# Differential attention in three units a head instead of four, with the filling products and the mixing dealt out anew

## The chip, the cores and the metric

The kernel runs on one core of one Trainium2 chip. The time is the device time of that core in microseconds (us); lower is better.

## The reference, cut to what matters

The kernel computes a trunk of two layers for one sequence of 512 tokens with 1024 features. A layer projects the normalized input into five parts, mixes two of them over time in chunks (the gating part), runs differential attention on the other three, and joins both with `w_out`; a convolved feed-forward part follows. Attention has 4 heads, and each head has two maps of 64 columns, whose softmaxes are subtracted. Queries come in blocks of 128 and see the keys up to their own block, so the four blocks of a head have 128, 256, 384 and 512 keys.

```python
u, v_sgu, q, k, v_att = jnp.split(proj, [...], axis=-1)
u = jax.nn.gelu(u)
v_sgu = jax.nn.gelu(v_sgu)
y_sgu = sgu_mixer(u, v_sgu, ...)     # u * (w @ rmsnorm(v_sgu) + b), chunks of 128, 4 groups
...
for start in range(0, S, Q_BLOCK):   # Q_BLOCK = 128, S = 512
    end = start + Q_BLOCK
    qb = q[:, start:end]
    kb = k[:, :end]
    scores = jnp.einsum('bqhmd,bkhmd->bhmqk', qb, kb) * scale
    scores = jnp.where(mask, scores, -jnp.inf)
    p = jax.nn.softmax(scores, axis=-1)
    attn = p[:, :, 0] - lam * p[:, :, 1]
    outs.append(jnp.einsum('bhqk,bkhd->bqhd', attn, v[:, :end]))
o = rmsnorm(jnp.concatenate(outs, axis=1), subln_g) * (1.0 - lambda_init)
...
h = h + jnp.concatenate([y_sgu, y_att], axis=-1) @ w_out[l]
h = h + conv_ffn(rmsnorm(h, ffn_norm[l]), ...)
```

## The kernel before, in words

**Products.** Every large product is made of rounded parts: an operand `x` is kept as a rounded `xh` and a remainder `xl`, and three products (`h*h`, `l*h`, `h*l`) are added up in one bank of TensorE's accumulator memory. Weight blocks arrive two ahead through SyncE's (SP's) queue as `raw`; ScalarE (ACT) copies them to `wh`, and VectorE (DVE), GpSimd (POOL) or a DMA makes the remainder `wl`. In the later part of a layer's blocks, those of `w_out` among them, GpSimd makes it in pieces of 512 columns.

**A unit of attention** is one head and one block of queries, written (head, block). Its work goes over the engines in turn: scores on TensorE (PE), `sc`, three pairs of products of 64 rows, one product of each pair for each map; a masked reduction to the smallest value `mn` on DVE, one for each map; two exponentials `s` on ACT, which also sum up; the difference of the two maps on DVE; transposes `at` on PE; a copy `aTh` on ACT and its remainder `aTl` on DVE; the value products `av` on PE; and a reduction on DVE that adds the two halves of `av` into `o`, the output of the head, and a square on ACT.

**A head's close.** After its four units, `out_rms` works out the norm of the head's rows with small operations on 4 columns in DVE, called root steps below (names `r0`, `ssq`, `or`). `out_norm` multiplies `o` with it; then `out_turn` transposes it (`ot`), `out_high` makes `yah` on ACT and `out_low` the remainder `yal` on DVE, and the products `wo` of `w_out` read both.

**Order.** A loop over `i` goes through the units of `todo`, and in step `i` each line works on another unit: scores of unit `i`, transposes of `u1` (unit `i-1`), values of `u2` (unit `i-2`), output of `u3` (unit `i-3`). Between them stand filling steps, `run(steps, n)`: six products of 512 columns each, or twelve of 256 for the values `va`, from the projections that the attention is still to use (`q`, `k`, `va` of heads 2 and 3, then the gating factors `u`, which are multiplied by DVE out of their banks and by ACT's gelu) and then from the first part of `w_out`. A filling step's side work waits in the lists `due` and `later`. The `mix` of the four gating groups (`mx`, twelve products, then `y` on DVE) stands at the iterations named by `MIX_AT`, `out_turn` of a head `HEAD_LATE` iterations after its last unit.

The order on each engine is pinned in the order in which the code issues (`pin`, through the objects `pe`, `act`, `dve`, `gps`, `sync`), so an instruction that waits holds up all that stand behind it on its engine. The exceptions are the small operations called as `nc.vector`, the root steps among them, which a scheduler places into DVE's order. Accumulator banks come from three pools in turn: `ps_mm` with 4 banks (`q`, `k`, `va`, `u`, `mx`, `wo`), `ps_sc` and `ps_tr` with 2 each.

Of the kernel before, what the change touches and what calls it, by code (L numbers as in the profile page):

```python
# [18 lines left out]
ALU = mybir.AluOpType  # L19
# [19 lines left out]
HEAD_LATE = 6  # L39
MIX_AT = (9, 10, 12, 13)  # L40
# [29 lines left out]
def trunk(ctx: ExitStack, tc, a, out):  # L70
# [420 lines left out]
    for l in range(DEPTH):  # L491
# [185 lines left out]
        class Unit:  # L677


            def __init__(self, h, qt, head):  # L680
                self.h, self.qt, self.n, self.head = h, qt, (qt + 1) * P, head
                self.name = f"{l}_{h}_{qt}"

            def scores(self):
                (qh, ql), (kh, kl) = qs[self.h], ks[self.h]
                n = self.n
                qsl = slice(n - P, n)
# [5 lines left out]
                self.mn = sm.tile([P, 2], F32, tag="mn", name=f"mn{self.name}")  # L693
                self.p = [tmp(f"s{self.name}_{c}") for c in range(2)]
                for c in range(2):
                    dve.tensor_tensor_reduce(
                        out=self.p[c][:, :n], in0=bk[c][:, :n], in1=mask[:, S - n :], op0=ALU.add, op1=ALU.min,
                        scale=-scale, scalar=3e38, accum_out=self.mn[:, c : c + 1],
                    )

            def exps(self):

                n, qt = self.n, self.qt
                for c in range(2):
                    p = self.p[c][:, :n]
                    act.activation(
                        p, p, AF.Exp, bias=self.mn[:, c : c + 1], scale=-1.0,
                        accum_out=self.head.esum[:, c, qt : qt + 1],
                    )

            def difference(self):

                n, qt = self.n, self.qt
                e0, e1 = [self.head.esum[:, c, qt : qt + 1] for c in range(2)]
                p0, p1 = [self.p[c][:, :n] for c in range(2)]
                cf = sm.tile([P, 2], F32, tag="cf", name=f"cf{self.name}")
                nc.vector.reciprocal(cf[:, 0:1], e1)
                nc.vector.scalar_tensor_tensor(cf[:, 1:2], e0, cf[:, 0:1], nlam, op0=ALU.mult, op1=ALU.mult)
                dve.scalar_tensor_tensor(p0, p1, cf[:, 1:2], p0, op0=ALU.mult, op1=ALU.add)

            def turn(self):
                self.bt = tr_bank(f"at{self.name}")
                for kt in range(self.qt + 1):
                    ksl = slice(kt * P, (kt + 1) * P)
                    transpose(self.bt[:, ksl], self.p[0][:, ksl], ident)
# [11 lines left out]
            def values(self):  # L737

                ah, al = self.a
                qt = self.qt  # L740
                self.bo = tr_bank(f"av{self.name}")
                for kt in range(qt + 1):
                    ksl = slice(kt * P, (kt + 1) * P)
                    v = va[kt][:, self.h]
                    mm(self.bo[:, : 2 * P], ah[:, ksl], v.rearrange("p x d -> p (x d)"), start=kt == 0, stop=False)
                    mm(self.bo[:, :P], al[:, ksl], v[:, 0], start=False, stop=kt == qt)
                self.o = self.head.o[:, qt * P : (qt + 1) * P]

            def out(self):
                dve.reduce_sum(self.o, self.bo[:, : 2 * P].rearrange("p (x d) -> p d x", x=2), axis=mybir.AxisListType.X)  # L750

            def out_square(self):
                sq = sm.tile([P, P], F32, tag="osq", name=f"osq{self.name}", bufs=2)
                act.activation(sq, self.o, AF.Square, accum_out=self.head.ssq[:, self.qt : self.qt + 1])
# [103 lines left out]
        todo = [(h, qt) for h in range(NH) for qt in range(NT)]  # L858
# [6 lines left out]
        for i in range(len(todo) + 2):  # L865
            u0 = None
            u1, u2, u3 = at(i - 1), at(i - 2), at(i - 3)
            ot = at(i - HEAD_LATE)
            if ot and ot.qt < NT - 1:
                ot = None  # L870
            if ot:
                ot.out_turn()
                ot.out_high()
            if u3:
                u3.out()
            if biased:
                biased.pop()()
            if i < len(todo):
                h, qt = todo[i]
                if qt == 0:  # L880
                    head = Head(h)
                units.append(Unit(h, qt, head))
                u0 = units[i]
                u0.scores()
# [21 lines left out]
            n3 = at(i - 4)  # L906
            if n3 and n3.qt == NT - 1:
                n3.out_norm()
# [6 lines left out]
            if i < 8:  # L915
                run(steps, 1)
# [294 lines left out]
```

## Time and profile before

| what | before |
|---|---|
| median of 3 runs | 1123.53 us (1123.48 to 1123.82) |
| the profiled execution: its time, its span | 1124.22 us, 1122.5 us |
| PE busy | 1110.7 us (99%) |
| DVE busy | 674.1 us (60%) |
| ACT busy | 494.3 us (44%) |
| POOL busy | 374.8 us (33%) |
| mean granted TensorE clock | 0.997 of full speed |
| largest queue of DMA | 28.7% of its 16 engines |

The span runs from the first instruction to the last of one profiled execution; its own time is 1.7 us longer. Busy shares are averages over all stages of the kernel. The products of PE overlap, so the times of single ones add up to more than the time they take; what a product costs is read from when it starts and when the next one starts.

### The profile page before, as it was taken

How to read it: one execution, taken by the hardware profiler on the slowest of the kernel's cores; microseconds unless marked ns; L12 is line 12 of the kernel's file. 1: busy time of each engine (PE TensorE's matmuls, PEld its weight loads, DVE VectorE, ACT ScalarE, POOL GpSimd, SP SyncE). 2: the span in 40 equal slices, each digit the busy share in tenths (PEclk: the TensorE clock that was granted, in tenths of full speed). 3: DMA queues.
4: the chain of work that ended last, by engine and by line, in shares of the span. 5: the costliest groups of instructions: out<-in, count | busy, mean ns of one | idle time of the engine just before them, and what ended most of it. 6: DMA issues, size and time to landing. Idle time of an engine off the chain costs nothing.

```text
span 1122.5 us, 14572 instructions
## 1 busy us (share of the span) xinstructions
PE 1110.7 (99%) x5459; PEld 925.3 (82%) x5459; DVE 674.1 (60%) x1242; ACT 494.3 (44%) x814; POOL 374.8 (33%) x370
## 2 busy tenths in 40 slices
PE   9999999999999999999999999999999999999996
PEld 7888888888888888888888788888888888888896
DVE  7778774766572146664328787677566522656634
ACT  5566554544442134443334764454444321444351
POOL 0533144333322113233556321452323211332351
PEclk9999999999999999999999999999999999999998
DMA  8175322333233223322333752222223322223322
GB/s 267 64 187 136 92 66 75 113 99 107 87 102 94 94 94 108 99 84 76 109 121 101 180 126 65 76 94 94 94 94 112 96 93 94 94 94 94 94 76 76
DMA packets 38694, 115.71 MB, mean 103 GB/s; under 512 B 4448, under 2 KB 10976, under 8 KB 38624
## 3 DMA queue, kind: packets, MB, share of 16 engines
q1 hardware_dynamic: 34224, 103.22, 28.7%
q0 software_dynamic: 2880, 10.49, 4.8%
q10 hardware_dynamic: 1520, 1.08, 0.3%
q8 instruction: 43, 0.70, 0.3%
q14 instruction: 27, 0.22, 0.1%
HBM read 102.19 MB, written 2.10 MB: 93 GB/s over the span
## 4 chain that ended last, share of the span: by engine, by line
PE 88%; DVE 6%; ACT 3%; issue 1%; POOL 1%; DMA 0%; SPq 0%; POOLq 0%; DVEq 0%; ACTq 0%
PE g L119 21%; PE v L119 21%; PE dn L119 19%; PE wo L119 7%; PE u L119 4%; PE vs L119 4%; PE dl L119 2%; PE va L119 2%; PE q L119 2%; PE av L119 1%; PE sc L119 1%; PE mx L119 1%; DVE s L119 1%; PE k L119 1%; ACT wh L119 1%
## 5 line engine op out<-in xcount | busy, mean ns | idle before, releaser
L119 POOL TENSOR_TENSOR wl<-raw,wh 128x512 fp32r<-128x512 f32 x147 | 201.9, 1394 | 515.8 <-ACT wh L119 515.7
L119 ACT CAST wh<-raw 128x1024 fp32r<-128x1024 f32 (+1 forms) x192 | 193.9, 1013 | 378.0 <-issue 182.8
L119 DVE TENSOR_TENSOR wl<-raw,wh 128x1024 fp32r<-128x1024 f32 (+1 forms) x96 | 121.0, 1260 | 131.8 <-ACT wh L119 131.4
L119 PE MATMUL v<-gh_f,wh 128*128 128x512 f32 x352 | 137.3, 390 | 0.0
L119 PE MATMUL v<-gh_f,wl 128*128 128x512 f32 x352 | 137.0, 389 | 0.0
L119 PE MATMUL g<-gh_f,wl 128*128 128x512 f32 x352 | 136.9, 389 | 0.0
L119 PE MATMUL g<-gh_f,wh 128*128 128x512 f32 x352 | 136.9, 389 | 0.0
L119 PE MATMUL g<-gl_f,wh 128*128 128x512 f32 x352 | 136.9, 389 | 0.0
L119 PE MATMUL v<-gl_f,wh 128*128 128x512 f32 x352 | 136.9, 389 | 0.0
L119 DVE SCALAR_TENSOR_TENSOR cv<-up_cv,par,cv 128x512 f32<-128x512 f32 x88 | 74.0, 885 | 6.4 <-ACT cv L119 6.1
L119 PEld LDWEIGHTS g<-gh_f,wh 128*128 128x128 f32 x352 | 66.1, 188 | 13.8
L119 PEld LDWEIGHTS v<-gh_f,wl 128*128 128x128 f32 x352 | 66.1, 188 | 13.7
L119 PEld LDWEIGHTS v<-gh_f,wh 128*128 128x128 f32 x352 | 66.1, 188 | 13.7
L119 PEld LDWEIGHTS g<-gh_f,wl 128*128 128x128 f32 x352 | 66.1, 188 | 13.7
L119 PEld LDWEIGHTS g<-gl_f,wh 128*128 128x128 f32 x352 | 66.1, 188 | 13.6
L119 PEld LDWEIGHTS v<-gl_f,wh 128*128 128x128 f32 x352 | 66.1, 188 | 13.6
L119 DVE SCALAR_TENSOR_TENSOR cg<-up_cg,par,cg 128x512 f32<-128x512 f32 x88 | 69.6, 841 | 6.0 <-ACT cg L119 5.6
L119 DVE TENSOR_TENSOR up_cv<-v,rstd_f 128x512 f32<-128x512 f32 x44 | 30.2, 692 | 67.3 <-PE v L119 67.2
L119 DVE TENSOR_TENSOR up_cg<-g,rstd_f 128x512 f32<-128x512 f32 x44 | 30.0, 692 | 57.8 <-PE g L119 54.9
L119 ACT ACTIVATE s<-s,mn 128x128 f32<-128x128 f32 (+3 forms) x64 | 35.5, 556 | 54.4 <-DVE mn L119 54.4
L119 ACT ACTIVATE cg<-cg 128x512 f32<-128x512 f32 x44 | 27.7, 630 | 45.8 <-DVE cg L119 45.8
L119 DVE TENSOR_TENSOR hT<-dn,hT 128x512 f32<-128x512 f32 x28 | 19.1, 691 | 47.2 <-PE dn L119 47.2
(620 smaller groups left out, 2562.8 us busy)
## 6 DMA issues: line engine op xcount, KB each, us to landing
raw<-in_w_up SPq DMA_DIRECT2D x88, 512.0 KB, 3.4
raw<-in_w_dn SPq DMA_DIRECT2D x40, 512.0 KB, 3.5
raw<-in_w_in SPq DMA_DIRECT2D x32, 512.0 KB, 3.6
wl<-raw POOLq DMA_DIRECT2D x20, 512.0 KB, 4.6
raw<-in_w_out SPq DMA_DIRECT2D x16, 512.0 KB, 3.4
hT<-in_xT SPq DMA_DIRECT2D x8, 256.0 KB, 4.6
or<-in_w_in SPq DMA_DIRECT2D x16, 128.0 KB, 4.4
raw<-in_w_dn SPq DMA_DIRECT2D x8, 256.0 KB, 3.1
```

The costliest lines, as they stand in the source:

```text
L119: return lambda *args, **kw: pin(getattr(self.engine, op)(*args, **kw))
```

## The change

The first two blocks of queries of a head become one unit. Its scores, 128 and 256 columns, lie side by side in one bank for each map, and so do its probabilities, its transposed maps and its outputs. Reductions, exponentials and differences are still done for each block, the larger one first; the copies `aTh` and `aTl`, the transposes' bank, and the reduction into `o` are done once for both. A layer has 12 units instead of 16, and 14 iterations instead of 18. An iteration has four filling steps for `i` below 6, three up to 9 and two after that, where it had three up to 7 and two after that. The mixings move to iterations 5, 7, 9 and 10. `out_norm` moves from the second half of an iteration to the start of the next one, and `out_turn` follows the last unit by 5 iterations. In the new code the root steps' lines lie 20 further down for `out_rms` and 2 for `rsqrt`.

```diff
-HEAD_LATE = 6
-MIX_AT = (9, 10, 12, 13)
+
+BLOCKS = ((0, 1), (2,), (3,))
+HEAD_LATE = 5
+MIX_AT = (5, 7, 9, 10)
...
-            def __init__(self, h, qt, head):
-                self.h, self.qt, self.n, self.head = h, qt, (qt + 1) * P, head
-                self.name = f"{l}_{h}_{qt}"
+            def __init__(self, h, qts, head):
+                self.h, self.qts, self.head = h, qts, head
+                ends = np.cumsum([(qt + 1) * P for qt in qts])
+                self.n = int(ends[-1])
+
+                self.blocks = [(qt, int(e) - (qt + 1) * P, (qt + 1) * P) for qt, e in zip(qts, ends)]
+                self.closes = qts[-1] == NT - 1
+                self.name = f"{l}_{h}_{qts[0]}"
...
                 for x, y, st, en in ((qh, kh, True, False), (qh, kl, False, False), (ql, kh, False, True)):
-                    for c in range(2):
-                        rows = slice(c * HD, (c + 1) * HD)
-                        mm(bk[c][:, :n], x[rows, qsl], y[rows, :n], start=st, stop=en)
...
+                    for qt, o, n in self.blocks:
+                        for c in range(2):
+                            rows = slice(c * HD, (c + 1) * HD)
+                            mm(
+                                bk[c][:, o : o + n], x[rows, n - P : n], y[rows, :n],
+                                start=st and o == 0, stop=en and qt == self.qts[-1],
+                            )
...
+                    for j, (qt, o, n) in reversed(list(enumerate(self.blocks))):
+                        dve.tensor_tensor_reduce(
+                            out=self.p[c][:, o : o + n], in0=bk[c][:, o : o + n], in1=mask[:, S - n :],
+                            op0=ALU.add, op1=ALU.min, scale=-scale, scalar=3e38, accum_out=self.mn[:, c, j : j + 1],
+                        )
...
-                nc.vector.reciprocal(cf[:, 0:1], e1)
-                nc.vector.scalar_tensor_tensor(cf[:, 1:2], e0, cf[:, 0:1], nlam, op0=ALU.mult, op1=ALU.mult)
-                dve.scalar_tensor_tensor(p0, p1, cf[:, 1:2], p0, op0=ALU.mult, op1=ALU.add)
+                k = len(self.qts)
...
+                nc.vector.reciprocal(cf[:, 0], e1)
+                nc.vector.scalar_tensor_tensor(cf[:, 1], e0, nlam, cf[:, 0], op0=ALU.mult, op1=ALU.mult)
+                for j, (qt, o, n) in enumerate(self.blocks):
+                    p0, p1 = [self.p[c][:, o : o + n] for c in range(2)]
+                    dve.scalar_tensor_tensor(p0, p1, cf[:, 1, j : j + 1], p0, op0=ALU.mult, op1=ALU.add)
...
-                dve.reduce_sum(self.o, self.bo[:, : 2 * P].rearrange("p (x d) -> p d x", x=2), axis=mybir.AxisListType.X)
+                k, q0 = len(self.qts), self.qts[0]
+                dve.reduce_sum(
+                    self.head.o[:, q0 * P : (q0 + k) * P].rearrange("p (t d) -> p t d", d=P),
+                    self.bo[:, : 2 * k * P].rearrange("p (t x d) -> p t d x", x=2, d=P),
+                    axis=mybir.AxisListType.X,
+                )
...
-        todo = [(h, qt) for h in range(NH) for qt in range(NT)]
+        todo = [(h, qts) for h in range(NH) for qts in BLOCKS]
...
-            ot = at(i - HEAD_LATE)
-            if ot and ot.qt < NT - 1:
-                ot = None
+            ot, n3 = [u if u and u.closes else None for u in (at(i - HEAD_LATE), at(i - HEAD_LATE + 1))]
             if ot:
                 ot.out_turn()
                 ot.out_high()
+            if n3:
+                n3.out_norm()
             if u3:
                 u3.out()
...
-                if u3.qt == NT - 1:
+                if u3.closes:
                     u3.out_rms()
...
-            n3 = at(i - 4)
-            if n3 and n3.qt == NT - 1:
-                n3.out_norm()
             if u2:
                 u2.values()
             if i in MIX_AT:
                 biased.append(mix(MIX_AT.index(i)))
             if later:
                 later.popleft()()
-            if i < 8:
-                run(steps, 1)
+            if i < 10:
+                run(steps, 2 if i < 6 else 1)
```

On PE the scores of head 1's first two blocks stand thus in layer 0 of the kernel before (`sc`, layer, head, block, map; columns at the end), the first block's group and the filling products behind it:

```order
L119 MATMUL sc0_1_0_0_1053<-k0_1h_860,q0_1h_633 128x128
L119 MATMUL sc0_1_0_1_1054<-k0_1h_860,q0_1h_633 128x128
L119 MATMUL sc0_1_0_0_1053<-k0_1l_861,q0_1h_633 128x128
L119 MATMUL sc0_1_0_1_1054<-k0_1l_861,q0_1h_633 128x128
L119 MATMUL sc0_1_0_0_1053<-k0_1h_860,q0_1l_634 128x128
L119 MATMUL sc0_1_0_1_1054<-k0_1h_860,q0_1l_634 128x128
L119 MATMUL k2_0_965<-gh4_a0_202,wh13_896 128x512
L119 MATMUL k2_0_965<-gl4_a0_203,wh13_896 128x512
L119 MATMUL k2_0_965<-gh4_a0_202,wl13_897 128x512
L119 MATMUL k3_0_966<-gh4_a0_202,wh13_896 128x512
```

and thus after the change:

```order
L121 MATMUL sc0_1_0_0_1032<-k0_1h_871,q0_1h_633 128x128
L121 MATMUL sc0_1_0_1_1033<-k0_1h_871,q0_1h_633 128x128
L121 MATMUL sc0_1_0_0_1032<-k0_1h_871,q0_1h_633 128x256
L121 MATMUL sc0_1_0_1_1033<-k0_1h_871,q0_1h_633 128x256
L121 MATMUL sc0_1_0_0_1032<-k0_1l_872,q0_1h_633 128x128
L121 MATMUL sc0_1_0_1_1033<-k0_1l_872,q0_1h_633 128x128
L121 MATMUL sc0_1_0_0_1032<-k0_1l_872,q0_1h_633 128x256
L121 MATMUL sc0_1_0_1_1033<-k0_1l_872,q0_1h_633 128x256
L121 MATMUL sc0_1_0_0_1032<-k0_1h_871,q0_1l_634 128x128
L121 MATMUL sc0_1_0_1_1033<-k0_1h_871,q0_1l_634 128x128
L121 MATMUL sc0_1_0_0_1032<-k0_1h_871,q0_1l_634 128x256
L121 MATMUL sc0_1_0_1_1033<-k0_1h_871,q0_1l_634 128x256
```

The second block's products of 256 columns, which stood in a group of their own behind fillings and other work, now stand between those of the first block, in one group of six pairs.

On DVE, at the end of layer 0's attention, this stood in the kernel before between the last root steps of head 2 (`or0_2_3`) and the last remainder `aTl`:

```order
L428 SCALAR_TENSOR_TENSOR or0_2_3_1858<-or0_2_3t_1859,or0_2_3_1858 128x4
L765 TENSOR_TENSOR or0_2_3_1858<-or0_2_3_1858,r00_2_3_1853 128x4
L717 RECIPROCAL cf0_3_3_1926<-esum0_3_1667 128x1
L718 SCALAR_TENSOR_TENSOR cf0_3_3_1926<-esum0_3_1667,cf0_3_3_1926,nlam0_806 128x1
L119 SCALAR_TENSOR_TENSOR s0_3_3_0_1899<-s0_3_3_1_1900,cf0_3_3_1926,s0_3_3_0_1899 128x512
L119 TENSOR_TENSOR aTl0_3_2_1924<-at0_3_2_1909,aTh0_3_2_1923 128x384
L119 TENSOR_TENSOR o0_2_1390<-o0_2_1390,or0_2_3_1858 128x512
L119 TENSOR_REDUCE o0_3_1666<-av0_3_1_1932 128x128
L119 TENSOR_TENSOR u2_0_1955<-u2_0_1682,rstd_a0_493 128x512
L119 TENSOR_TENSOR u3_0_1972<-u3_0_1683,rstd_a0_493 128x512
L119 TENSOR_TENSOR aTl0_3_3_1975<-at0_3_3_1957,aTh0_3_3_1974 128x512
```

After the change this stands there; the first piece ends with three of the root steps behind `aTl` of unit (3,2),

```order
L121 SCALAR_TENSOR_TENSOR s0_3_3_0_1816<-s0_3_3_1_1817,cf0_3_3_1862,s0_3_3_0_1816 128x512
L782 TENSOR_TENSOR ssq0_2_1375<-ssq0_2_1375,r00_2_3_1834 128x4
L121 TENSOR_TENSOR aTl0_3_2_1860<-at0_3_2_1826,aTh0_3_2_1859 128x384
L783 TENSOR_SCALAR ssq0_2_1375<-ssq0_2_1375 128x4
L425 TENSOR_SCALAR or0_2_3_1839<-ssq0_2_1375 128x4
L426 TENSOR_SCALAR ssq0_2_1375<-ssq0_2_1375 128x4
```

and after eight further root steps the second piece goes on:

```order
L430 SCALAR_TENSOR_TENSOR or0_2_3_1839<-or0_2_3t_1840,or0_2_3_1839 128x4
L785 TENSOR_TENSOR or0_2_3_1839<-or0_2_3_1839,r00_2_3_1834 128x4
L121 TENSOR_TENSOR o0_2_1373<-o0_2_1373,or0_2_3_1839 128x512
L121 TENSOR_REDUCE o0_3_1636<-av0_3_0_1867 128x256
L121 TENSOR_TENSOR u2_0_1893<-u2_0_1617,rstd_a0_493 128x512
L121 TENSOR_TENSOR u3_0_1912<-u3_0_1618,rstd_a0_493 128x512
L121 TENSOR_TENSOR aTl0_3_3_1915<-at0_3_3_1895,aTh0_3_3_1914 128x512
```

The root steps of head 2, which ended ahead of the difference `s0_3_3`, now stand behind `aTl0_3_2`, thirteen in a row with nothing between them, and the reduction of head 3 that follows is that of its first two blocks.

On DVE, where the bank of the first mixing is emptied (`y0_0` reads `mx0_0`), this stood in layer 0 before, at head 2's second and third block (`s0_2_1`, `s0_2_2`):

```order
L119 SCALAR_TENSOR_TENSOR s0_2_1_0_1475<-s0_2_1_1_1476,cf0_2_1_1503,s0_2_1_0_1475 128x256
L119 TENSOR_TENSOR aTl0_2_0_1501<-at0_2_0_1488,aTh0_2_0_1500 128x128
L119 TENSOR_REDUCE o0_1_1050<-av0_1_3_1508 128x128
L119 SCALAR_TENSOR_TENSOR y0_0_1531<-mx0_0_1517,par_93,bsb0_281 128x512
L119 ISA s0_2_2_0_1542,mn0_2_2_1541<-sc0_2_2_0_1533,mask_115 128x384
```

and this stands there after the change, at head 0's close:

```order
L430 SCALAR_TENSOR_TENSOR or0_0_3_1287<-or0_0_3t_1288,or0_0_3_1287 128x4
L785 TENSOR_TENSOR or0_0_3_1287<-or0_0_3_1287,r00_0_3_1282 128x4
L121 TENSOR_TENSOR o0_0_811<-o0_0_811,or0_0_3_1287 128x512
L121 TENSOR_REDUCE o0_1_1029<-av0_1_0_1325 128x256
L121 SCALAR_TENSOR_TENSOR y0_0_1371<-mx0_0_1332,par_93,bsb0_281 128x512
L121 ISA s0_2_0_0_1391,mn0_2_0_1390<-sc0_2_0_0_1376,mask_115 128x256
```

`y0_0` moved ahead, from the scores of head 2's third block to those of its first two, and stands behind the last root steps and the normalization of head 0 and the reduction of head 1's first two blocks.

## Rows read from the trace of the kernel before

**Rows 1.** Busy time by stretch, in layer 0 (columns as in the header).

```profile
84.00:105.00 21.00, 20.56 (x144) 17.35 (x143) 18.99 (x59) 14.31 (x34) 9.77 (x9) 1.00 0.53 137
```

**Rows 2.** PE's waits, whole run: total us, times, longest.

```profile
PE at L119 <- DVE aTl L119: 1.0, 2, 0.6
```

**Rows 3.** Timeline of PE: start us, us, operation, [idle before].

```profile
84.12 0.39 PE L119 MATMUL k<-gl_a,wh 128*128 128x512 f32 x1
84.34 0.40 PE L119 MATMUL k<-gh_a,wl 128*128 128x512 f32 x1
84.67 0.33 PE L119 MATMUL sc<-k_1h,q_1h 64*128 64x128 f32 x2
84.84 0.28 PE L119 MATMUL sc<-k_1l,q_1h 64*128 64x128 f32 x2
84.95 0.28 PE L119 MATMUL sc<-k_1h,q_1l 64*128 64x128 f32 x2
...
85.50 0.39 PE L119 MATMUL k<-gl_a,wh 128*128 128x512 f32 x1
```

**Rows 4.** Timeline of PE, the next score group.

```profile
91.27 0.39 PE L119 MATMUL sc<-k_1h,q_1h 64*128 64x256 f32 x2
91.50 0.28 PE L119 MATMUL sc<-k_1l,q_1h 64*128 64x256 f32 x2
91.61 0.28 PE L119 MATMUL sc<-k_1h,q_1l 64*128 64x256 f32 x2
...
92.16 0.40 PE L119 MATMUL k<-gl_a,wh 128*128 128x512 f32 x1
```

**Rows 5.** Chain that ended last, pieces from 103 us: start, us, what.

```profile
103.03 0.89 PE sc L119 x6
...
105.55 0.33 PE at L119 x3
105.88 1.44 PE va L119 x12
```

**Rows 6.** The same chain, a mixing of layer 0.

```profile
140.90 1.34 PE mx L119 x12
```

**Rows 7.** Timeline of DVE, the remainder in unit (1,3).

```profile
108.73 0.55 DVE L119 TENSOR_TENSOR aTl<-at,aTh 128x384 fp32r<-128x384 f32 x1
```

**Rows 8.** Timeline of DVE, first and last of thirteen root steps.

```profile
101.95 0.16 DVE L763 TENSOR_SCALAR ssq<-ssq 128x4 f32<-128x4 f32 x1
...
104.31 0.16 DVE L765 TENSOR_TENSOR or<-or,r 128x4 f32<-128x4 f32 x1
```

**Rows 9.** Timeline of all engines, end of attention in layer 0.

```profile
146.27 0.50 PE L119 MATMUL sc<-k_3h,q_3h 64*128 64x512 f32 x2
...
151.08 0.55 DVE L119 TENSOR_TENSOR aTl<-at,aTh 128x384 fp32r<-128x384 f32 x1
...
151.55 3.09 POOL L119 TENSOR_TENSOR wl<-raw,wh 128x512 fp32r<-128x512 f32 x2 [8.06 <-ACT wh L119]
...
153.84 0.29 ACT L119 ACTIVATE osq<-o 128x128 f32<-128x128 f32 x1
...
154.13 0.57 ACT L119 CAST aTh<-at 128x512 fp32r<-128x512 f32 x1
...
158.34 0.75 DVE L119 SCALAR_TENSOR_TENSOR yal<-ot,sgain,yah 128x512 fp32r<-128x512 f32 x1 [0.60 <-ACT yah L119]
...
158.80 0.44 PE L119 MATMUL wo<-yah,wh 128*128 128x512 f32 x1
...
159.14 0.19 PEld L119 LDWEIGHTS wo<-yal,wh 128*128 128x128 f32 x1 [0.21 <-DVE yal L119]
```

**Rows 10.** Timeline of all engines, while GpSimd makes remainders.

```profile
165.68 2.53 POOL L119 TENSOR_TENSOR wl<-raw,wh 128x512 fp32r<-128x512 f32 x2 [2.80 <-ACT wh L119]
165.69 1.29 DVE L428 SCALAR_TENSOR_TENSOR or<-or_3t,or 128x4 f32<-128x4 f32 x1
...
167.02 1.21 DVE L426 TENSOR_TENSOR or_3t<-ssq,or 128x4 f32<-128x4 f32 x1
```

More of the change, by code (lines that the diff above doesn't have):

```diff
@@ L701, in exps @@
             def exps(self):
-                n, qt = self.n, self.qt
                 for c in range(2):
[L705 to L709, printed above, removed]
-            def difference(self):
[L713 to L716, printed above, removed]
-                nc.vector.reciprocal(cf[:, 0:1], e1)
-                nc.vector.scalar_tensor_tensor(cf[:, 1:2], e0, cf[:, 0:1], nlam, op0=ALU.mult, op1=ALU.mult)
-                dve.scalar_tensor_tensor(p0, p1, cf[:, 1:2], p0, op0=ALU.mult, op1=ALU.add)
+                    for j, (qt, o, n) in reversed(list(enumerate(self.blocks))):
+                        p = self.p[c][:, o : o + n]
+                        act.activation(
+                            p, p, AF.Exp, bias=self.mn[:, c, j : j + 1], scale=-1.0,
+                            accum_out=self.head.esum[:, c, qt : qt + 1],
+                        )
@@ new lines, in difference @@
+            def difference(self):
+                k = len(self.qts)
+                e0, e1 = [self.head.esum[:, c, self.qts[0] : self.qts[0] + k] for c in range(2)]
+                cf = sm.tile([P, 2, k], F32, tag=f"cf{k}", name=f"cf{self.name}")
+                nc.vector.reciprocal(cf[:, 0], e1)
[3 more added lines that the diff above has]
+                    dve.scalar_tensor_tensor(p0, p1, cf[:, 1, j : j + 1], p0, op0=ALU.mult, op1=ALU.add)
@@ L721, in turn @@
             def turn(self):
                 self.bt = tr_bank(f"at{self.name}")
[L723 to L725 removed]
+                for o in range(0, self.n, P):
+                    transpose(self.bt[:, o : o + P], self.p[0][:, o : o + P], ident)
             def high(self):
@@ L739, in values @@
                 ah, al = self.a
[L740 removed]
                 self.bo = tr_bank(f"av{self.name}")
[L742 to L747, printed above, removed]
[L749 to L754 removed]
+                for j, (qt, o, n) in enumerate(self.blocks):
+                    left = 2 * j * P
+                    for kt in range(qt + 1):
+                        ksl = slice(o + kt * P, o + kt * P + P)
+                        v = va[kt][:, self.h]
+                        b = self.bo[:, left : left + 2 * P]
+                        mm(b, ah[:, ksl], v.rearrange("p x d -> p (x d)"), start=kt == 0, stop=False)
+                        mm(b[:, :P], al[:, ksl], v[:, 0], start=False, stop=kt == qt)
+            def out(self):
+                k, q0 = len(self.qts), self.qts[0]
[3 more added lines that the diff above has]
+                    axis=mybir.AxisListType.X,
+                )
+            def out_square(self):
+                for qt in self.qts:
+                    sq = sm.tile([P, P], F32, tag="osq", name=f"osq{l}_{self.h}_{qt}", bufs=2)
+                    act.activation(
+                        sq, self.head.o[:, qt * P : qt * P + P], AF.Square, accum_out=self.head.ssq[:, qt : qt + 1]
+                    )
             def out_rms(self):
```

14 lines of the change are left out of this document (4 added, 10 removed).

## The prediction

> **What bounds the kernel now.** I began with the page's busy shares, which put TensorE (PE) far ahead of the other engines. The share of a stretch says more, so I cut out the attention of layer 0: from 84 to 105 us PE is busy 20.56 of 21.00 us at a granted clock of 1.00 (2.4 GHz), while VectorE (DVE) is busy 18.99 of 21.00 [rows 1]. PE is the bound and DVE is right behind it. The list of PE's waits then says how little there is to win by removing waits: in the whole attention one kind counts, two waits of 1.0 us together for a remainder `aTl` from DVE [rows 2]. So a gain has to come from what the products themselves cost PE, and a loss can come from anything that makes DVE late. I read both from start times, since the durations of PE's products overlap.
>
> **What the change saves on PE.** The count of products stays the same. What goes is one score group a head: the entry into a group of 64-row products and the way out of it. Two filling products follow each other in 0.22 to 0.23 us (84.12 to 84.34). From the filling product ahead of a 128-column group to the second one behind it, 84.34 to 85.50, is 1.16 us; less two spacings the group costs 0.70. For 256 columns it is 0.89 from the first pair to the second filling product, 91.27 to 92.16; with the same 0.33 ahead (84.34 to 84.67) and less two spacings it costs 0.76 [rows 3, 4]. Within a group the second pair starts 0.17 us after the first (84.67, 84.84), and the later pairs follow in 0.11 whether they have 128 columns (84.84, 84.95) or 256 (91.50, 91.61). The joint group has six pairs: 0.33 in, 0.17, four times 0.115, then 0.20 out and 0.35 to the second filler, less 0.46, which is 1.05. It saves 0.41 a head, 3.3 us for eight heads. Transposes, value products and mixing products cost the same in other groups. Some of it is given back: before, seven score groups a layer stand directly behind other short products and now three do; each such neighbourhood spares one change between short products and fillers, which I estimate from the same entry and exit gaps at 0.07, so 0.6 in all. Net **-2.7 us**.
>
> Here a page speaks against the change: the Trainium skill, TensorE: Matmul & The Clock Gate, section "The mechanism" under "Part 3: Packing small matmuls", says that a weight load overlaps with running products only when its row group differs. All pairs of a group use the same two row groups, so by that page each later pair would wait as the second one does. The trace of this case disagrees: the later pairs come after 0.11 us, not 0.17. What it would cost is the third rival.
>
> **The old waits.** Both waits of [rows 2] stand ahead of the transposes of unit (0,3), one in each layer; to their 1.0 us I add 0.15 each for PE's way back into its pace, an estimate of the size of the entry gaps above. With four filling steps instead of three between these scores and their transposes PE comes 1.4 us later, and DVE no longer has these scores' reductions behind a rotary shuffle. Both waits go: **-1.3 us**.
>
> **A new wait at `u1`.** The mixing of group 0 now stands at step 5, and the bank of `mx0` is given to `u1`, whose first product in step 6 must wait for `y0`, the DVE operation that empties it. PE's way from the scores of head 1's last block to that product: scores 0.89, two value steps at 1.44 with the transposes 0.33 between (3.4 with the re-entry), six value products at about 0.1, mixing 1.34, two more steps 2.9, the joint scores 0.9 and three products of `u0` 0.8, together 10.8 us [rows 5, 6]. DVE: `aTl` ended 6.3 us after these scores began in the kernel before (103.03, 108.73 and 0.55) [rows 5, 7]. Now one `k` remainder (0.6) and five root steps stand ahead of it. A root step is one of the 4-column operations of head normalization; thirteen take 2.53 us, 101.95 to 104.47, 0.195 each [rows 8]. So `aTl` ends at about 7.7; then nine root steps 1.8, the normalization of `o` and the reduction of a double output block at 0.65 and 0.7 and `y0` at 0.75 (the width of `yal` in [rows 9]) give 11.4. PE waits 0.5 us a layer; between 0, if DVE's gaps swallow the root steps, and 1.2, if none does. **+1.0 us.**
>
> **A new wait at the end of attention.** This term decides. Before, the root of head 2 was spread over two iterations, in gaps where DVE waited for exponentials. Now `out_rms` comes in step 11 and `out_norm` opens step 12, so thirteen root steps stand in a row between `aTl` of unit (3,2) and `o`. Behind `o` stands the reduction of head 3's first two blocks, and ScalarE's (ACT's) two squares of that reduction stand, in its own queue, ahead of the copy `aTh` of the last transposes. From there the path is the old one: in the kernel before, `aTh` began at 154.13 and the last link, `yal` of head 2, ended at 159.09, 4.96 us later; PE needed `yal` at 159.14 [rows 9]. That path had no room: the weight load of PE's second `wo` product, 0.34 us after the first, waited for `yal`.
>
> Counted from the start of the last scores (146.27): `aTl` ends at about 5.0 (151.63, or 5.4, before, when root steps still delayed the scores' reductions by some 0.3). Thirteen root steps would end at 7.5. But at 5.3 GpSimd begins two weight remainders (151.55, two in 3.09 us, one of them held by DVE). What that does to root steps is seen 14 us later: while GpSimd worked on two remainders from 165.68, two root steps took 1.29 and 1.21 us instead of 0.16 [rows 10]. Two of the thirteen held so add 2.2, so they end at 9.7. `o` 0.65 and the reduction 0.7 make 11.0, two squares at 0.29 make 11.6, and the old path of 4.96 makes 16.5. PE needs `yal` at 13.0: the first `wo` product came at 12.53 before, value products of three instead of two key blocks in step 11 add 0.23, and `yal` is read about 0.28 later (0.34 less a part of that load's wait). PE waits **3.5 us a layer**. Without the hold `yal` is there at 14.3 and the wait is 1.3; these are the bounds. Both layers have the same order: **+7.0 us**. On the way, `wo2` waits for DVE to empty `u2`, but that lies inside the same 3.5.
>
> The other moves cost nothing: the remaining transposes and value products have at least 0.7 us between DVE's last step and PE by the same kind of count (the tightest is the first unit, where four exponentials instead of two add 1.0 us on ACT and PE comes 1.9 later). If that cover were gone, each would cost PE what is missing, at most some tenths. Weight blocks are asked for at the same pace, four filling steps to a block, and no queue is passed.
>
> **Sum.** -2.7 - 1.3 + 1.0 + 7.0 = +4.0 us. The profiled execution took 1124.22 us for its span of 1122.5; the change is added to it, 1128.2, and since the median of the runs is 0.7 lower, to that: **1127.5 us**.
>
> **Rivals.**
> - *The roots are not held up* (23%). DVE slips more root steps between GpSimd's two operations. For it: the holds seen are whole operations, but where they fall depends on tenths of a microsecond. Then the tail costs 2.6 and the sum is -0.4: 1123.1 us, no change.
> - *The new waits stay covered* (14%). What decides is when `o` of head 2 is normalized: up to 6.8 us after the last scores began, the old path of 4.96 still meets PE at 13.0, counting reduction and squares. For it: DVE had idle time ahead of `aTh`'s remainder, since ACT was the late one there. Against it: thirteen steps from 5.0 end at 7.5 even unheld. Then only the savings count, 4.0 less: 1119.5 us, faster.
> - *Score pairs do not run on* (5%). Each later pair of a joint group waits like the second pair of a group: 0.17 behind 128 columns, 0.23 behind 256 (91.27 to 91.50), so the five gaps are 0.97 instead of 0.63 and eight groups lose 2.7: 1130.2 us. The later gaps in [rows 3, 4] speak against it.
> - *More is late* (8%): `u1` waits 1.2 in each layer and a third root step is held for 1.1, 1.8 us more in each layer: 1131.1 us.
>
> **How the numbers follow.** Half the chance is on the forecast, whose own range is 1125.8 to 1129.3. About 0.2% (2.2 us) is what a measurement of this kernel can tell from no change. Slower by more than that holds the forecast and the last two rivals, 0.63; the same is the first rival, 0.23; faster is the second, 0.14. The range that leaves out the faster case and the last, 2 in 10, is 1122.4 to 1130.4.
>
> **What would show it.** The profile after should have joint score groups with gaps of 0.11 to 0.12 from the third pair on, about 1.05 us each; no wait ahead of the transposes of (0,3) in either layer; a wait of PE at `u` for DVE `y` of up to 1 us a layer; and the largest new wait at `wo` for DVE `yal` or ACT `yah` (part of it at `wo` for `u`), 1.3 to 3.5 us a layer, with a string of 4-column steps on DVE of which two last over 1 us. If `o` of head 2 is ready within 6.8 us of the last scores, the largest term is wrong and the kernel is faster.

## The result, and the profile after

The changed kernel takes 1130.18 us (median of 6 runs, 1129.26 to 1132.13) against 1123.89 us of the kernel before, a ratio of 1.0057 with a 95% interval of 1.0047 to 1.0067: it is slower by 6.3 us. Its profiled execution took 1129.26 us with a span of 1127.5, so 5.0 more than before.

Where the time went can be read by following the same products through both executions, since the filling products come in the same order. The table has the start of some of them, in us (one ahead of each layer's attention, the first `wo` product, and the second one behind the values of unit (3,3), which reads `yal` of head 2).

| product | before | after | after less before |
|---|---|---|---|
| `q`, ahead of layer 0's attention | 30.55 | 29.95 | -0.60 |
| first `wo`, layer 0 | 150.81 | 149.16 | -1.65 |
| `wo` behind the last values, layer 0 | 159.14 | 162.09 | +2.95 |
| `k`, ahead of layer 1's attention | 600.11 | 602.98 | +2.87 |
| first `wo`, layer 1 | 702.14 | 703.88 | +1.74 |
| `wo` behind the last values, layer 1 | 710.50 | 715.71 | +5.21 |

Attention gains 1.1 us in each layer, and then its end loses 4.6 in layer 0 and 3.5 in layer 1. The list of PE's waits names what it loses to. It replaces [rows 2]: the two waits for `aTl` are gone, and there are four for `o` and one for `yal` (us in total, times, longest).

```profile
PE av L121 <- DVE o L121: 6.8, 4, 2.8
...
PE wo L121 <- DVE yal L121: 0.3, 1, 0.3
```

The timeline of all engines at the end of layer 0's attention answers to [rows 9]. The columns are the start in us, the duration, engine, line, operation, tiles, and the idle time before with what ended it.

```profile
144.42 0.49 PE L121 MATMUL sc<-k_3h,q_3h 64*128 64x512 f32 x2
...
148.90 0.55 DVE L121 TENSOR_TENSOR aTl<-at,aTh 128x384 fp32r<-128x384 f32 x1
...
149.62 2.55 POOL L121 TENSOR_TENSOR wl<-raw,wh 128x512 fp32r<-128x512 f32 x2 [7.12 <-ACT wh L121]
...
149.77 1.17 DVE L426 TENSOR_SCALAR ssq<-ssq 128x4 f32<-128x4 f32 x1
...
150.97 1.22 DVE L428 TENSOR_TENSOR or_3t<-ssq,or 128x4 f32<-128x4 f32 x1
...
153.80 0.16 DVE L785 TENSOR_TENSOR or<-or,r 128x4 f32<-128x4 f32 x1
154.00 0.69 DVE L121 TENSOR_TENSOR o<-o,or 128x512 f32<-128x512 f32 x1
154.61 0.68 DVE L121 TENSOR_REDUCE o<-av 128x256 f32<-128x512 f32 x1
...
155.44 0.36 PE L121 MATMUL av<-va,aTh 128*128 128x256 f32 x1 [2.85 <-DVE o L121]
...
155.99 0.56 ACT L121 CAST aTh<-at 128x512 fp32r<-128x512 f32 x1
...
160.19 0.75 DVE L121 SCALAR_TENSOR_TENSOR yal<-ot,sgain,yah 128x512 fp32r<-128x512 f32 x1 [0.60 <-ACT yah L121]
```

The last scores start at 144.42. DVE's remainder `aTl` of unit (3,2) ends at 149.45. Then come the thirteen root steps; GpSimd starts two remainders at 149.62, and the two root steps beside them take 1.17 and 1.22 us instead of 0.16. The string ends at 153.96, `o` at 154.69, the reduction at 155.29. PE has stood since its product of 152.19, and goes on at 155.44 with the values of unit (3,2): their bank is the one that this reduction empties. In layer 1 the same wait is 2.84 us.

Behind that wait in layer 0, though not in layer 1, PE's clock was lower. The table by stretch has the granted clock in the third column from the end.

```profile
core 0: us, PE busy (x) PEld busy (x) DVE busy (x) ACT busy (x) POOL busy (x), PEclk, DMA share, GB/s
152.60:155.40 2.80, 0.00 (x0) 0.00 (x0) 2.53 (x10) 0.01 (x1) 0.00 (x0) 1.00 0.60 187
155.40:157.00 1.60, 1.56 (x11) 1.59 (x11) 1.50 (x3) 1.15 (x5) 0.00 (x0) 0.70 0.00 0
157.00:159.00 2.00, 2.00 (x7) 1.61 (x6) 1.31 (x3) 1.09 (x3) 0.00 (x0) 0.50 0.00 0
...
710.00:712.00 2.00, 1.85 (x13) 1.77 (x14) 1.90 (x5) 1.17 (x5) 0.00 (x0) 1.00 0.00 0
```

The wait stands between two products that start 3.25 us apart. Behind it the clock stays at 1.00 (2.4 GHz) up to 156.0 and is 0.50 (1.2 GHz) from 156.2 to 159.4; the 0.70 is the mean of a stretch with both. From the first product behind the wait to the seventh `wo` product PE takes 4.13 us in layer 0 (155.44 to 159.57) and 2.55 in layer 1 (710.15 to 712.70), so the lower clock cost it 1.6 us. Layer 0 loses only 1.1 more than layer 1, because PE came to `yal` later by it and didn't have to wait there, as it did in layer 1 (0.29). The Trainium skill, TensorE: Matmul & The Clock Gate, section "What's actually happening", says that the gate's watching runs on by itself and doesn't start anew with the kernel. The trace is in keeping with that, since the same wait is followed by 1.00 in layer 1 (710 to 712), but it doesn't show why the two layers differ. The runs of this kernel with a mean clock of 0.996 took 1129.3, those with 0.994 1130.1 to 1131.0, and the one with 0.992 1132.1; the median lies 0.9 above the profiled execution.

### The profile page after: what moved, and what is told of

It reads as the page before. It is cut to its first block, busy times and chain, and to the rows that moved or that the text cites. A ratio compares the mean times of both kernels' runs of the same rounds, so it can differ in the third digit from the quotient of the medians.

```text
span 1127.5 us, 14498 instructions
## 1 busy us (share of the span) xinstructions
PE 1109.6 (98%) x5459; PEld 925.3 (82%) x5459; DVE 683.1 (61%) x1210; ACT 493.0 (44%) x806; POOL 373.6 (33%) x370
## 3 DMA queue, kind: packets, MB, share of 16 engines
q10 hardware_dynamic: 1520, 1.08, 0.3%
## 4 chain that ended last, share of the span: by engine, by line
PE 93%; DVE 4%; ACT 1%; issue 1%; POOL 0%; POOLq 0%; ACTq 0%; DVEq 0%
PE g L121 21%; PE v L121 21%; PE dn L121 19%; PE wo L121 7%; PE va L121 4%; PE k L121 4%; PE q L121 4%; PE vs L121 4%; PE u L121 2%; PE dl L121 2%; PE sc L121 2%; PE av L121 1%; PE mx L121 1%; PE at L121 1%; ACT s L121 0%
## 5 line engine op out<-in xcount | busy, mean ns | idle before, releaser
L121 ACT ACTIVATE s<-s,mn 128x256 f32<-128x256 f32 (+2 forms) x64 | 35.3, 554 | 31.2 <-DVE mn L121 30.9
```

Source lines behind the costliest of these rows:

```text
L121: return lambda *args, **kw: pin(getattr(self.engine, op)(*args, **kw))
```

## The experiments

Two theories stood against each other. **A:** the loss is the string of root steps on DVE, its length and the place where it stands. **The rivals:** it is only the order of two pinned operations (theory B), or the shortness of the iterations that get fewer filling steps (C), or a lack of time on DVE wherever the steps stand. All times are medians, and a ratio is that to the kernel before on the same chip, which took 1123.8 to 1124.0.

| run | us | ratio, 95% interval |
|---|---|---|
| changed kernel | 1130.18 | 1.0057 [1.0047, 1.0067] |
| 1 remainders by DMA | 1122.77 | 0.9992 [0.9982, 1.0001] |
| 2 reduction ahead of the root | 1129.90 | 1.0053 [1.0038, 1.0068] |
| 3 fillings dealt later | 1125.48 | 1.0014 [1.0004, 1.0023] |
| 4 four units in the new code | 1123.92 | 1.0001 [0.9991, 1.0010] |
| 5 one round of Newton | 1124.55 | 1.0006 [0.9996, 1.0015] |
| 6 edits 1 and 3 | 1127.88 | 1.0036 [1.0023, 1.0048] |
| 7 edit 1 in the kernel before | 1126.16 | 1.0020 [1.0011, 1.0029] |
| 8 squares first | 1130.96 | 1.0069 [1.0053, 1.0084] |
| 9 squares first, edit 3 | 1125.76 | 1.0018 [1.0009, 1.0026] |
| 10 and gelu later | 1123.30 | 0.9995 [0.9987, 1.0004] |
| 11 the same, squares behind gelu at the end | 1120.98 | 0.9973 [0.9963, 0.9984] |
| 12 squares of run 11 alone | 1124.12 | 1.0002 [0.9993, 1.0011] |

**1. Does GpSimd stretch the string?** Blocks of this kind have a second way to their remainder, which takes GpSimd's arithmetic away.

```diff
-            if 10 <= i_l < 20:
+            if 10 <= i_l < 23:
```

> The changed kernel, with the remainders wl of the first three blocks of w_out (made by GpSimd before) made as those of the later w_in blocks are: ACT writes the negative, a DMA adds the raw block. GpSimd then does nothing beside the root steps of heads 1 and 2. Theory A (thirteen root steps in a row on DVE, two of them stretched to 0.9 to 1.2 us by GpSimd, stand ahead of out_norm and of the reduction that empties the bank of av): all root steps take about 0.2, the reduction ends 2.1 us earlier, PE's wait at av falls from 2.85 to about 0.8 in each layer, about 0.6 more shows at wo for yal, the wait of 0.55 one head earlier goes, and the clock no longer falls behind the wait: 1123 to 1125 us. Rival: the stretched steps are not what PE waits for, or ACT's three more passes a layer delay the copies aTh as much: 1129 to 1131 us.

It took 1122.77, a little below the lower end. The timeline at the same place, counted here from last scores at 143.88, has every root step at 0.16, and the reduction ends 8.8 us after the scores instead of 10.9:

```profile
151.20 0.16 DVE L785 TENSOR_TENSOR or<-or,r 128x4 f32<-128x4 f32 x1
...
152.01 0.68 DVE L121 TENSOR_REDUCE o<-av 128x256 f32<-128x512 f32 x1
...
152.84 0.35 PE L121 MATMUL av<-va,aTh 128*128 128x256 f32 x1 [0.77 <-DVE o L121]
```

PE's wait is 0.77 in place of 2.85, and one head earlier there is none. The Trainium skill, SBUF — State Buffer, section "SBUF: two separate sides", says that GpSimd and a DVE operation with two inputs in that memory, or in certain modes, share a pair of ports; whichever starts first holds the pair for its whole instruction, and the other one blocks. The stretched steps agree: in the changed kernel the second one ends at 152.19, and GpSimd's pair at 152.17. The first of them has one input only, and no run here shows in which mode it ran. The rival, that it isn't the stretched steps, fell.

**7. Is that gain the edit's own?** The same line in the kernel before.

> The kernel before with the remainders of the first three blocks of w_out by DMA: what that edit is worth without the change. By theory A nothing, since the kernel before has no string of root steps ahead of work that PE waits for: 1123 to 1124.5 us. If it is below 1122.5, the gain of the two kernels with this edit is its own and not a loss taken back.

It isn't: there the edit costs 2.2 us, which I hadn't expected. ACT's three more passes a layer make PE wait for `yah`, 1.1 in all, and for `yal`, 0.6:

```profile
PE wo L119 <- ACT yah L119: 1.1, 2, 0.6
...
PE wo L119 <- DVE yal L119: 0.6, 2, 0.3
```

So the 7.4 us between run 1 and the changed kernel are a loss taken back, not a gain of the edit's own.

**2. Is it only the bank?** The reduction is put ahead of the root steps, which are pinned behind it (the lines that pin them are left out here).

```diff
-            if n3:
-                n3.out_norm()
             if u3:
                 u3.out()
+            if n3:
+                n3.out_rms()
+                n3.out_norm()
...
-                if u3.closes:
-                    u3.out_rms()
```

> The changed kernel, with the reduction of av put ahead of the root steps and of out_norm (the root is issued, pinned, where out_norm stands). Theory A (the root steps' length on DVE sets PE's wait, and the bank of av is only where it shows first): the wait of 2.85 at av goes, but o of head 2 is ready as late as before, so PE waits some 2.3 us at ot for o or soon behind it at wo for yal, 3.0 to 3.8 in all in each layer: 1128.5 to 1131 us. Theory B (the order of two pinned operations is the whole loss, the bank being held behind out_norm): all the waits go, 1122.5 to 1125 us.

It took 1129.90: counted from the last scores (144.99) the bank is free 5.2 us earlier, and nothing is won. The wait stands at `ot`, for the `o` that comes out of the string:

```profile
149.94 0.69 DVE L121 TENSOR_REDUCE o<-av 128x256 f32<-128x512 f32 x1
...
150.75 2.01 DVE L121 TENSOR_TENSOR ssq<-ssq,r 128x4 f32<-128x4 f32 x2
...
155.37 0.69 DVE L121 TENSOR_TENSOR o<-o,or 128x512 f32<-128x512 f32 x1
...
156.11 1.11 PE L121 MATMUL ot<-ident,o 128*128 128x128 f32 x4 [2.29 <-DVE o L121]
```

PE waits 2.29 there, 0.3 for `yal` in one layer, and up to 0.7 at `u` for `y` in each, the wait that the prediction had feared, since the whole string now stands, pinned, ahead of `y0`. Part of this is the edit's own: all sixteen root steps stand behind the reduction, where three of them had been done before it, two of them again stretched (150.75), so `o` is ready 11.1 us after the last scores instead of 10.3. These 0.8 us explain only a part of the 2.29, and theory B had all waits go, so it fell: the bank is where the string shows first, not the cause.

**5. Is it the length?** The root of heads 0 to 2 gets one round of three, so six steps of each string are left out.

```diff
-        for _ in range(3):
+        for _ in range(rounds):
...
-                self.r = rsqrt(ssq, NT, f"or{self.name}")
+                self.r = rsqrt(ssq, NT, f"or{self.name}", 3 if self.h == NH - 1 else 1)
```

> The changed kernel with one round of Newton's iteration instead of three in the root of heads 0 to 2, so that their normalization is inexact: six root steps of about 0.2 us fewer in each head's close, everything else as changed. Theory A (PE's waits are as long as DVE's string of root steps): the wait of 0.55 at av one head earlier goes with its way back (0.75), the waits at the end fall by 1.2, to 1.65 at av and to about 2.3 in all in each layer, two stretched steps stay: 3.9 less than the changed kernel and up to 1 less from the clock, 1125 to 1126.5 us. Rival (only the two steps stretched by GpSimd matter, the others fill time that DVE has): no more than 0.5 less, 1129 to 1130.5 us.

It took 1124.55, 5.6 less than the changed kernel and a little below the range. The wait left at `av` is the one that was counted, 1.6 in each layer; with 0.3 at `wo` it is 1.9 in all, less than the 2.3:

```profile
PE av L121 <- DVE o L121: 3.3, 2, 1.6
...
PE wo L121 <- DVE yal L121: 0.6, 2, 0.3
```

**3. Can PE be made to come later?** One filling step more goes into each of iterations 10 and 11, one less into each of 6 and 7.

```diff
-            if i < 10:
+            if i < 6 or i > 7 and i < len(todo):
                 run(steps, 2 if i < 6 else 1)
```

> The changed kernel with the same 16 filling steps of the gates dealt as two in iterations 6 and 7 and three in 8 to 11, instead of three in 6 to 9 and two in 10 and 11. DVE's work is as before; PE comes one filling step (1.4 us) later to the values of heads 1's and 2's close. Theory A and its kin: the wait of 0.55 goes, the waits at the end fall by 1.4 to about 2.1 in each layer: 1125 to 1127.5 us. Rival C (the two shorter iterations lack the time for their own unit): new waits of 0.7 to 1.4 at at or av in iterations 7 and 8, 1128 to 1131 us.

It took 1125.48. The wait one head earlier is gone, and that at the end fell from 2.85 to 1.58, with no new one in iterations 7 and 8; one of 0.3 at `ot` in iteration 10 and 0.3 at `wo` for `yal` came up. The string came earlier against GpSimd's work, so that other operations were stretched:

```profile
150.22 2.54 POOL L121 TENSOR_TENSOR wl<-raw,wh 128x512 fp32r<-128x512 f32 x2 [7.42 <-ACT wh L121]
...
150.26 1.27 DVE L785 TENSOR_TENSOR or<-or,r 128x4 f32<-128x4 f32 x1
...
151.57 1.74 DVE L121 TENSOR_TENSOR o<-o,or 128x512 f32<-128x512 f32 x1
...
154.06 0.36 PE L121 MATMUL av<-va,aTh 128*128 128x256 f32 x1 [1.58 <-DVE o L121]
```

The last root step takes 1.27 and the normalization of `o` 1.74 instead of 0.69. The same 2 us are lost there, so the hold isn't one of root steps in particular. Rival C fell.

**4. Does the new code cost anything by itself?** Four units a head, with the old `HEAD_LATE`, `MIX_AT` and dealing.

```diff
-BLOCKS = ((0, 1), (2,), (3,))
-HEAD_LATE = 5
-MIX_AT = (5, 7, 9, 10)
+BLOCKS = ((0,), (1,), (2,), (3,))
+HEAD_LATE = 6
+MIX_AT = (9, 10, 12, 13)
...
-            if i < 10:
-                run(steps, 2 if i < 6 else 1)
+            if i < 8:
+                run(steps, 1)
```

> The changed kernel's code with four units a head again, and the old HEAD_LATE, MIX_AT and dealing: what is left of the change is out_norm at the start of an iteration instead of the end of the one before, and the code of a unit. By every theory here within 0.2% of the kernel before, 1122.5 to 1124.8 us, with the old two waits for aTl of 0.5 us each. If it is above 1126 the place of out_norm costs by itself.

1123.92, as expected: neither the code of a unit nor `out_norm` at the start of an iteration costs anything that shows where the root has two iterations.

**6. Both cures.**

> The changed kernel with both: remainders of the first three blocks of w_out by DMA, and the gates' filling steps dealt later. By theory A the string is 2.1 us shorter and PE comes 1.4 later, which is all that the waits at the end came to (3.5): PE waits less than 0.4 in each layer there, none one head earlier, and what the joint groups save on PE shows: 1119.3 to 1121 us, faster than the kernel before by 0.25 to 0.4%. Rival (the joint unit costs something else that these waits hid): not under 1121.5 us.

It took 1127.88, far from what theory A gave. The waits at `av` are gone, but PE now waited for what ACT makes, as in run 7. Its timeline behind the last scores (143.62):

```profile
149.99 1.06 ACT L121 ACTIVATE wl<-raw 128x1024 fp32r<-128x1024 f32 x1 [2.45 <-PE u L121]
...
152.01 1.28 ACT L121 ACT_TABLE_LOAD   x1
...
154.94 0.56 ACT L121 CAST aTh<-at 128x512 fp32r<-128x512 f32 x1
...
158.44 0.67 ACT L121 ACTIVATE yah<-ot,sgain 128x512 fp32r<-128x512 f32 x1
...
159.16 0.50 PE L121 MATMUL wo<-yah,wh 128*128 128x512 f32 x1 [1.27 <-ACT yah L121]
```

The extra pass at 149.99 pushes the table load, `gelu` and the copy `aTh` back; `yah` is ready at 159.11 and PE waits 1.27 for it. One head earlier another such pass, at 131.52, stands ahead of `aTh`, and PE waits 1.30 at `ot` behind it. In layer 0 the clock fell behind these waits, to 0.55 from 161 to 163 us. So the rival's number was right, by a cause of the cure and not of the joint unit.

**8, 12. Is it the place?** ACT squares `o` ahead of the exponentials of the scores, not behind them. The scheduler then puts the same string ahead of the last scores' reductions. Run 8 has this for all iterations; run 12, whose edit is shown, only where there are scores:

```diff
+            if u3 and u0:
+                u3.out_square()
+                if u3.closes:
+                    u3.out_rms()
             if u0:
                 u0.exps()
             elif i == len(todo):
                 gelu(0)
                 gelu(1)
-            if u3:
+            if u3 and not u0:
                 u3.out_square()
-                if u3.closes:
-                    u3.out_rms()
```

> The changed kernel with ACT's squares of a unit's output issued ahead of the exponentials instead of behind them, so that the same root steps of head 2 stand on DVE ahead of the reductions of the last scores, some 3 us earlier, and no longer between aTl and out_norm. Nothing is made shorter. Theory A (the place of the string): no wait for o at av; the last unit's reductions and differences come some 2.5 us later, of which PE has 1.7 in hand, so a wait of 0.5 to 1.5 shows at the last transposes, in place of the 3.5 in each layer: 1122.5 to 1125.5 us. Rival (DVE simply lacks the time at the end, wherever the steps stand): the last unit's transposes wait about as long as av did, 1128.5 to 1130.5 us.

Run 8 took 1130.96, above either of my ranges. Its timeline shows the expected wait of 1.13 at the last transposes, and a second one that my edit brought:

```profile
151.35 0.66 PE L121 MATMUL at<-ident,s 128*128 128x128 f32 x4 [1.13 <-DVE aTl L121]
...
152.72 0.68 DVE L121 TENSOR_REDUCE o<-av 128x256 f32<-128x512 f32 x1
...
154.21 1.28 ACT L121 ACT_TABLE_LOAD   x1
...
156.56 0.57 ACT L121 CAST aTh<-at 128x512 fp32r<-128x512 f32 x1
...
160.78 0.50 PE L121 MATMUL wo<-yah,wh 128*128 128x512 f32 x1 [1.74 <-ACT yah L121]
```

In the iteration behind the last scores the squares wait for the reduction at 152.72, and the table load and two gelus stand behind them on ACT, so that `aTh` came at 156.56. Run 12 keeps that iteration as it was.

> The changed kernel with the squares ahead of the exponentials while there are scores to reduce, and behind gelu of u0 and u1 in the iteration after; nothing else. The run with the squares first everywhere, without its side effect on the table load. Theory A (the place of the string): its wait of about 1.1 at the last transposes stays, the waits of 1.7 and 0.3 at wo go, so 1.1 to 1.6 in each layer instead of 3.5, and none one head earlier: 1124.5 to 1127 us. Rival (DVE lacks the time at the end wherever the steps stand): the waits at wo stay, 1129 us or more.

It took 1124.12, 6.1 less than the changed kernel, with no step left out. PE's waits in the whole run:

```profile
PE at L121 <- DVE aTl L121: 2.3, 2, 1.1
...
PE wo L121 <- DVE yal L121: 0.6, 2, 0.3
```

1.4 us in each layer, as theory A counted, and 0.2 more at `av` in one. The rival that DVE lacks the time wherever the steps stand fell. But the edit doesn't change the place alone, since in its new place the string misses GpSimd's pair. No root step of head 2 is stretched, and the pair holds up the normalization of `o` instead:

```profile
147.44 0.16 DVE L785 TENSOR_TENSOR or<-or,r 128x4 f32<-128x4 f32 x1
...
151.39 1.59 DVE L121 TENSOR_TENSOR o<-o,or 128x512 f32<-128x512 f32 x1
```

That is 0.9 us lost where the changed kernel loses 2.1, in each layer. How much of the 6.1 us is the place and how much the shorter holds, no run separates.

**9, 10, 11. A version that keeps the saving.** Run 9 is run 8 with the later dealing, run 10 has `gelu` of `u2` and `u3` behind `yah` besides, and run 11 is that with the squares as in run 12.

```diff
                 gated(0)
-                gelu(2)
-                gelu(3)
+        gelu(2)
+        gelu(3)
         end = units[-1]
```

> The changed kernel with the squares first and the gates' filling steps dealt later. By theory A the last unit's transposes no longer wait, and what can be left is a reduction stretched by GpSimd and the way to yal, up to 1 us in each layer: 1119.8 to 1122 us. Rival (shorter iterations 6 and 7 have no room for the string of head 0 in its new place): above 1122.5 us, with waits at at or u there.

> As the run before, with ACT's gelu of u2 and u3 behind yah of head 2 instead of ahead of it, so that yah and yal come about 1.1 us earlier. By theory A PE waits less than 0.5 in each layer and what the change saves on PE is left, 4 us in all: 1119.3 to 1121 us, faster than the kernel before by 0.25% or more. If the yal path is not what is left, it takes the same time as the run before.

> As the run with three edits, but in the first iteration behind the last scores ACT's squares stay behind gelu of u0 and u1, so that the table load does not wait for head 3's reduction. The copy aTh of the last transposes then comes about 2 us earlier, and yal before PE wants it. By theory A the waits of 0.6 and 0.2 at wo go and up to 0.3 at ot is left in each layer: 1120.5 to 1122 us, 0.15 to 0.3% faster than the kernel before. If it is not under 1122.5, something other than these waits holds back what the joint groups save.

Run 9 took 1125.76: PE waited 1.2 for `yah` and 0.3 for `yal` in each layer, the table load of run 8 again; its rival fell too, since there was no wait at `at` or `u` in iterations 6 and 7. Run 10 took 1123.30, 2.3 above the range, with 0.6 for `yal` left in each layer and 0.2 for `yah` in one. Run 11 removed these and took 1120.98, faster than both kernels (0.27% than the one before, interval 0.16 to 0.37%). Of PE's waits in attention one of 0.2 is left, at `ot`; the others are those of the kernel's start and end:

```profile
PE ot L121 <- DVE u L121: 0.2, 1, 0.2
```

## Why the prediction was right

The forecast was 1127.5 with a range of 1122.4 to 1130.4; the median is 1130.18. Sign and mechanism were right: the string of root steps, two of them held by GpSimd, cost what it was said to cost. The total is in part luck. The median lies outside the forecast's own range (1125.8 to 1129.3), and only 0.2 below the upper end of the wide one. By the number alone it is nearer to the third and the fourth rival (1130.2 and 1131.1), but the trace has neither: the later pairs run on, `u1` doesn't wait, and no third root step is held at the end. Point by point:

- **The saving on PE and the old waits** (-2.7 and -1.3): right. Without the waits of 0.58 and 0.54 at `av` one head earlier and PE's way back behind them (0.25 each, estimated from the starts around 134.14), layer 0 gains 1.9 and layer 1 1.9, together 3.8. The joint group shows as summed; a row of `sc` is two pairs here:

```profile
83.29 0.39 PE L121 MATMUL k<-gh_a,wl 128*128 128x512 f32 x1
83.61 0.50 PE L121 MATMUL sc<-k_1h,q_1h 64*128 64x128 f32 x4
83.95 0.39 PE L121 MATMUL sc<-k_1l,q_1h 64*128 64x128 f32 x4
84.17 0.39 PE L121 MATMUL sc<-k_1h,q_1l 64*128 64x128 f32 x4
...
84.83 0.39 PE L121 MATMUL k<-gl_a,wh 128*128 128x512 f32 x1
```

- From the filling product ahead of it to the second one behind it are 1.54 us, less two spacings of 0.23 that is 1.08, summed as 1.05. From the third pair to the fifth are 0.22, two gaps of 0.11: score pairs run on, and the rival in which they don't fell.
- **The wait at `u1`** (+1.0): wrong, there is none. `y` ends at 109.80 and PE wants the bank at 110.11, 10.9 us after the scores, as summed (10.8).

```profile
109.06 0.74 DVE L121 SCALAR_TENSOR_TENSOR y<-mx,par,bsb 128x512 f32<-128x512 f32 x1
...
110.11 0.40 PE L121 MATMUL u<-gh_a,wh 128*128 128x512 f32 x1
```

- `aTl` was 0.8 us earlier than I had it, since root steps fell into DVE's gaps. This is the lower bound that the step named. Its sum has a slip too: 6.3, 0.6 and five steps make 7.9 and not 7.7, and from 7.7 its terms come to 11.6 and not 11.4; by its own rows the wait would have been 0.8 to 1.0 a layer. Run 2 shows the wait where the steps are pinned: 0.7.
- **The wait at the end** (+7.0): right to 0.1 us in size in layer 1, 3.5; the 4.6 of layer 0 have the clock in them. From the start of the last scores the sum had the string end at 9.7, the reduction at 11.0, the squares at 11.6, `yal` at 16.5; measured were 9.5, 10.9, 11.6 and 16.5. But its place was wrong: 2.85 of it stood at `av` and only 0.3 at `wo` in one layer. The size came out all the same, because the path to `yal` still ended last in layer 1, 0.3 after PE wanted it. The step that failed is "the remaining transposes and value products have at least 0.7 us". It counted `aTl` against PE, and left out that `av` also waits for the bank that the reduction empties.
- **One head earlier** that same step missed a loss: head 1's string is stretched by GpSimd too, and the bank comes late in each layer.

```profile
128.14 2.52 POOL L121 TENSOR_TENSOR wl<-raw,wh 128x512 fp32r<-128x512 f32 x2 [7.43 <-ACT wh L121]
...
128.53 0.93 DVE L425 TENSOR_SCALAR or<-ssq 128x4 int32<-128x4 int32 x1
...
129.49 1.21 DVE L426 TENSOR_SCALAR ssq<-ssq 128x4 f32<-128x4 f32 x1
...
134.14 0.36 PE L121 MATMUL av<-va,aTh 128*128 128x256 f32 x1 [0.58 <-DVE o L121]
```

- That is 0.58 and 0.54 of waiting, some 1.6 us with the way back, and takes the place of the 1.0 that was not lost at `u1`. That these two errors largely cancel is luck.
- **What the sum had no term for** is the clock behind the long wait: 1.1 us net in the profiled execution. With the 0.9 by which the median lies above that execution, it is most of what the median lies above the forecast (2.7); that these 0.9 are the clock too rests on the mean clocks alone.
- **The rivals.** Unheld roots: run 1 shows that state on DVE, and the changed kernel wasn't in it. Covered waits: the point named was `o` normalized within 6.8 us of the last scores; it was 10.3. With the waits covered, in run 11, the time is 1121.0, where this rival gave 1119.5.

## What to carry to other kernels

When work units are merged, the chains that ran once a unit keep their length but get fewer iterations to hide in; count the small operations that a scheduler may string together ahead of a pinned one, and look for what stands behind that one, banks to be emptied as well as data. A faster product stream is worth nothing if a string of operations of 0.2 us then meets it, and moving its input earlier brought back 6 us here, in part because the string then missed GpSimd's work. Look at each engine's own queue before trusting a cure: an edit that freed DVE here loaded ACT, and the second cure's squares held up a table load.

## What the runs showed of the hardware that I had not expected

- A DVE operation on 4 columns took 1.2 us instead of 0.16, and one on 512 columns 1.74 instead of 0.69, while GpSimd made its remainders; two such operations at the end of each layer's attention made DVE 2.1 us late there, 4.2 in both layers, and the change's savings came to 3.8.
- The same wait of 2.85 us was followed by 3.2 us at a granted clock of 0.50 (156.2 to 159.4) in one layer and by 1.00 in the other. The lower clock cost PE 1.6 us, 1.1 net, more than the wait itself shows; no run shows why one layer had it and the other not.
- ACT's table load of 1.28 us waits with the instructions behind it for a square that stands ahead of it in ACT's pinned order (it starts at 154.21 in run 8, at 149.56 in the changed kernel): where it stands made 1.7 us of PE's waiting in each layer (runs 8 and 12).
